# A routing stage whose order of experts, round count and weights are computed behind the token table

## The chip, the cores and the metric

The kernel runs on one core of a Trainium2 chip. The metric is the device time of one execution in microseconds. The kernel before takes 2070.55 us (median of 3 runs, 2066.29 to 2071.88).

## The reference

Two transformer blocks over 1024 tokens of width 1024. The first block has attention (a dilated and a neighbourhood branch) and a two-level mixture of 16 experts: the best of 4 groups, then the best 2 of its 4 experts. The second has three recurrent mixers and a feed-forward part. The change touches only the routing of the mixture:

```
g_weight, g_idx = lax.top_k(jax.nn.softmax(g_logits, axis=-1), 1)
e_in_group = jnp.take_along_axis(e_logits, g_idx[:, :, None], axis=1)[:, 0]
e_val, e_idx = lax.top_k(e_in_group, TOP_K_EXPERT)
e_weight = jax.nn.softmax(e_val, axis=-1) * g_weight
expert_id = g_idx * EXPERTS_PER_GROUP + e_idx
...
act = jax.nn.silu(gate) * up * combine[:, :, None].astype(x.dtype)
out = jnp.einsum('nef,efd->nd', act, w_down)
```

The kernel computes only the chosen experts: each expert gets the rows of the tokens that chose it.

## The kernel before

The attention output is projected in tiles of 128 tokens (`out_and_route`). Behind each tile the router's logits are made, and `route` handles the tokens in two batches of four tiles. From comparisons it makes one-hot rows `oh` (first and second choice), a running count of tokens per expert (`pk`, a matmul with a triangle of ones) and from it each token's rank `rk`. Two matmul groups (L899) then turn one-hot rows and ranks into the token table `tab`: for each expert (column) and each slot (row) the number of the token that sits there.

Behind the second batch come these pieces, all on VectorE:

- `sort_experts`: the load of each expert, its `place` when experts are sorted by load, the permutation `perm`, and `order`, the expert that stands at each place (L921 and L923).
- `sort_tokens`: `ix` from the table, `ixp` (table times permutation) and `idx`, the token numbers for each place (L936, L937); then `cmx` and `nround`, the number of rounds (L939 to L947).
- `route_weights`: expert ids `eid` and the softmax weights `wt` (L846 to L859).
- `slots_main`: `slot` and `wv`, where each token finds its results and with which weight (L956 to L976).

Two of these results start transfers. `idx` is read by GpSimd, which gathers token rows from DRAM by an indirect DMA (`xg<-xn_d,idx`, L1062): one for each tile of a job, into three buffers. `order` is read by SyncE into a register (L1054), which is the expert whose weights are then loaded (`wraw`, L227, 512 KB each): four units of gate and up weights and two of down weights for each expert, into four buffers. ScalarE casts each unit to a rounded high part `whi` (L237), VectorE subtracts to get the low part `wlo` (L238). A gathered tile is transposed on TensorE (L278) into two PSUM banks, copied by ScalarE (`XgH`, L280) and subtracted by VectorE (`XgL`, L281); each product is three matmuls (L260, L261, L262: high by high, low by high, high by low).

Every engine runs its instructions in one fixed order. That order is not the order of the code: when the program is built, instructions are ordered by what they depend on and by when their inputs are expected, so code of several functions is interleaved on VectorE. A read of a value that stands behind another instruction is what holds a piece back.

In the text below, W0 to W3 are the four gate and up units of the first expert, W4 and W5 the first two of the second expert, g0 and g1 the first two gathered tiles (both for the first expert), g2 the third.

Of the kernel before, what the change touches and what calls it, by code (L numbers as in the profile page):

```python
# [7 lines left out]
F32 = mybir.dt.float32  # L8
# [4 lines left out]
OP = mybir.AluOpType  # L13
AX = mybir.AxisListType
# [172 lines left out]
class K:  # L187
# [650 lines left out]
    def route_weights(self, wk, LG, oh):  # L838

        nc, V = self.nc, self.nc.vector  # L840
        e16 = self.rc[:, 144:160]
        w = wk.tile([128, 8, 20], F32, name="rwk")
        t3 = wk.tile([128, 8, 2, 16], F32, name="rt3")
        wg = w[:, :, 0:4]
        col = lambda i: w[:, :, 8 + i]
        V.tensor_tensor(t3, oh, e16[:, None, None, :].to_broadcast([128, 8, 2, 16]), op=OP.mult)  # L846
        V.tensor_reduce(self.eid, t3, axis=AX.X, op=OP.add)
        V.tensor_reduce(col(0), LG[:, :, 0:4], axis=AX.X, op=OP.max)
        V.tensor_tensor(wg, LG[:, :, 0:4], col(0).unsqueeze(2).to_broadcast([128, 8, 4]), op=OP.subtract)
        nc.scalar.activation(wg, wg, AF.Exp)  # L850
        V.tensor_reduce(col(3), wg, axis=AX.X, op=OP.add)
        V.tensor_tensor(t3, oh, LG[:, :, None, 4:20].to_broadcast([128, 8, 2, 16]), op=OP.mult)
        V.tensor_reduce(w[:, :, 9:11], t3, axis=AX.X, op=OP.add)
        V.tensor_tensor(col(4), col(2), col(1), op=OP.subtract)
        nc.scalar.activation(col(4), col(4), AF.Exp)
        V.tensor_scalar(col(5), col(4), 1.0, None, op0=OP.add)
        V.tensor_tensor(col(5), col(5), col(3), op=OP.mult)
        V.reciprocal(self.wt[:, :, 0], col(5))
        V.tensor_tensor(self.wt[:, :, 1], self.wt[:, :, 0], col(4), op=OP.mult)  # L859
# [46 lines left out]
    def sort_experts(self, wk, pc):  # L906

        nc, V = self.nc, self.nc.vector
        e16 = self.rc[:, 144:160]
        ab = lambda v: v.unsqueeze(2).to_broadcast([128, 16, 16])  # L910
        bb = lambda v: v[:, None, :].to_broadcast([128, 16, 16])
        load = wk.tile([128, 16], F32, name="load")
        key = wk.tile([128, 16], F32, name="key")
        V.scalar_tensor_tensor(key, pc, 16.0, e16, op0=OP.mult, op1=OP.subtract)
        t = wk.tile([128, 16, 16], F32, name="cmp")
        V.tensor_tensor(t, bb(key), ab(key), op=OP.is_gt)
        self.place = wk.tile([128, 16], F32, name="place")
        V.tensor_reduce(self.place, t, axis=AX.X, op=OP.add)
        perm = self.perm = wk.tile([128, 16, 16], F32, name="perm")
        V.tensor_tensor(perm, bb(self.place), ab(e16), op=OP.is_equal)  # L920
        V.tensor_tensor(t, perm, bb(e16), op=OP.mult)  # L921
        self.order = self.wp.tile([128, 16], I32, name="order")
        V.tensor_reduce(self.order, t, axis=AX.X, op=OP.max)  # L923
        V.tensor_copy(load, pc)
        self.load = load

    def sort_tokens(self, wk):

        V = self.nc.vector
        bb = lambda v: v[:, None, :].to_broadcast([128, 16, 16])  # L930
        self.idx = self.wp.tile([128, 2, 16], I32, name="idx")
        ix = wk.tile([128, 2, 16], F32, name="ix")
        ixp = wk.tile([128, 2, 16, 16], F32, name="ixp")
        V.tensor_tensor(ix, self.tab[:, :, 0:16], self.tab[:, :, 16:32], op=OP.add)
        for s in range(2):
            V.tensor_tensor(ixp[:, s], self.perm, bb(ix[:, s]), op=OP.mult)  # L936
            V.tensor_reduce(self.idx[:, s], ixp[:, s], axis=AX.X, op=OP.max)  # L937
        cm = wk.tile([128, 16], F32, name="cmx")
        V.tensor_scalar(cm, self.place, 0.5, None, op0=OP.is_ge)  # L939
        V.scalar_tensor_tensor(cm, self.place, NMORE + 0.5, cm, op0=OP.is_ge, op1=OP.add)  # L940
        V.scalar_tensor_tensor(cm, cm, 64.0, self.load, op0=OP.mult, op1=OP.add)
        V.tensor_reduce(cm[:, 0:1], cm, axis=AX.X, op=OP.max)
        V.tensor_scalar(cm[:, 1:2], cm[:, 0:1], 256.5, None, op0=OP.is_ge)
        for x in (512.5, 768.5, 1024.5):
            V.tensor_scalar(cm[:, 2:3], cm[:, 0:1], x, None, op0=OP.is_ge)
            V.tensor_tensor(cm[:, 1:2], cm[:, 1:2], cm[:, 2:3], op=OP.add)
        V.tensor_scalar(self.nround, cm[:, 1:2], 1.0, None, op0=OP.add)  # L947
# [1326 lines left out]
```

## Time and profile before

| | |
|---|---|
| median of the runs | 2070.55 us |
| the profiled execution's own time | 2072.83 us |
| its span | 2071.0 us |
| TensorE busy | 1933.4 us (93%) |
| VectorE busy | 1333.4 us (64%) |
| ScalarE busy | 931.1 us (45%) |
| mean DMA rate | 160 GB/s |
| mean granted clock | 0.97 |

The span is the profiled part of one execution; the time of the run is a little longer. Times below are microseconds from the span's start. An engine's busy share is a mean over stages with different limits, so the stage of the change is read by itself. In a row of instructions the bracket tells how long the engine stood idle before it and what ended the idle time.

### The profile page before, as it was taken

The page shows a single profiled execution, that of the slowest core. Times are in us where ns is not written, and L with a number is a line of the kernel's source. Part 1 is how long each engine was busy: PE and PEld are TensorE (multiplying, and loading weights), DVE is VectorE, ACT ScalarE, POOL GpSimd, SP SyncE. Part 2 cuts the span into 40 slices and gives each one's busy share as a digit, 9 for nine tenths or more (in the row PEclk, how much of TensorE's full clock was granted, in tenths as well). Part 3 has the DMA queues.
Part 4 walks back from the last instruction along what each step waited for, and adds up shares of the span by engine and source line. Part 5 has one row for each costly group of instructions (what it writes and reads, how often), then busy time and mean ns, then how long its engine had stood idle before and what let it go on. Part 6 is the DMA issues. An engine that isn't in the chain of part 4 may idle for free.

```text
span 2071.0 us, 27616 instructions
## 1 busy us (share of the span) xinstructions
PE 1933.4 (93%) x9481; PEld 1524.1 (74%) x9481; DVE 1333.4 (64%) x2670; ACT 931.1 (45%) x1648; POOL 731.3 (35%) x721
## 2 busy tenths in 40 slices
PE   8999999999899699995999989997999999999998
PEld 6877777776678577764887657675888888888886
DVE  4146667555657677766468278888667667675555
ACT  4245555444433477764422373454333333344344
POOL 2111102333442111105455224215677777740130
PEclk9999999999999799997999998998999999999999
DMA  6153322233332799966434246633335435458664
GB/s 243 61 130 101 89 76 79 87 103 102 114 127 83 251 315 317 319 239 219 166 97 68 72 165 206 201 133 133 141 134 180 148 135 182 149 193 305 195 190 167
DMA packets 161220, 332.23 MB, mean 160 GB/s; under 512 B 26256, under 2 KB 71600, under 8 KB 160560
## 3 DMA queue, kind: packets, MB, share of 16 engines
q1 hardware_dynamic: 139520, 260.64, 38.5%
q0 software_dynamic: 18848, 68.43, 10.1%
q10 hardware_dynamic: 2704, 1.31, 0.3%
q8 instruction: 77, 1.26, 0.3%
q14 instruction: 71, 0.58, 0.1%
HBM read 235.88 MB, written 84.93 MB: 155 GB/s over the span
## 4 chain that ended last, share of the span: by engine, by line
PE 40%; DVE 6%; POOL 3%; issue 3%; DMA 2%; ACT 1%; SPq 0%; POOLq 0%; DVEq 0%; ACTq 0%
PE pd L260 3%; PE pd L262 3%; PE pd L261 3%; PE pb L260 3%; PE pb L262 3%; PE pb L261 3%; PE pa L262 2%; PE pa L260 2%; PE pc L260 2%; PE pc L261 2%; PE pc L262 2%; PE pa L261 2%; PE pvg L260 1%; PE pvg L262 1%; PE pvg L261 1%
## 5 line engine op out<-in xcount | busy, mean ns | idle before, releaser
L2001 ACT CAST whi<-wraw 128x1024 fp32r<-128x1024 f32 x137 | 134.7, 984 | 273.7 <-PE pd L262 89.1
L2002 DVE TENSOR_TENSOR wlo<-wraw,whi 128x1024 fp32r<-128x1024 f32 x137 | 178.3, 1303 | 78.1 <-ACT whi L2001 75.9
L237 ACT CAST whi<-wraw 128x1024 fp32r<-128x1024 f32 x122 | 127.9, 1049 | 120.1 <-PE pp L261 37.8
L260 PE MATMUL pp<-XH,whi 128*128 128x512 f32 x416 | 167.2, 402 | 1.0 <-DVE kk L404 0.9
L262 PE MATMUL pp<-XH,wlo 128*128 128x512 f32 x416 | 165.8, 398 | 0.0
L261 PE MATMUL pp<-XL,whi 128*128 128x512 f32 x416 | 165.3, 397 | 0.0
L238 DVE TENSOR_TENSOR wlo<-wraw,whi 128x1024 fp32r<-128x1024 f32 x96 | 117.3, 1223 | 52.0 <-ACT whi L237 50.8
L238 POOL TENSOR_TENSOR wlo<-wraw,whi 128x1024 fp32r<-128x1024 f32 x26 | 63.1, 2427 | 172.6 <-ACT whi L237 163.6
L260 PE MATMUL pd<-whi 128*128 128x512 f32 x308 | 120.2, 391 | 1.0 <-DVE res L2171 0.9
L261 PE MATMUL pd<-wlo,whi 128*128 128x512 f32 x308 | 120.3, 390 | 0.5 <-DVE wlo L2002 0.5
L262 PE MATMUL pd<-whi,wlo 128*128 128x512 f32 x308 | 120.1, 390 | 0.0
L1062 POOL DMA_INDIRECT xg<-xn_d,idx x25 | 31.8, 1272 | 180.6 <-PE pt L278 141.3
L260 PEld LDWEIGHTS pp<-XH,whi 128*128 128x128 f32 x416 | 78.8, 189 | 19.5 <-issue 3.6
L262 PEld LDWEIGHTS pp<-XH,wlo 128*128 128x128 f32 x416 | 78.8, 189 | 15.5 <-issue 1.4
L261 PEld LDWEIGHTS pp<-XL,whi 128*128 128x128 f32 x416 | 78.8, 190 | 15.1 <-issue 1.5
L531 ACT ACTIVATE PP<-PP,stat 128x256 f32<-128x256 f32 x128 | 64.5, 504 | 39.6 <-DVE stat L529 37.5
L529 DVE CUSTOM_DVE_ANT_0 PP<-sp,bias 128x256 f32<-128x256 f32 x128 | 52.9, 422 | 25.5 <-PE sp L527 21.3
L281 DVE TENSOR_TENSOR XL<-pt,XH 128x512 fp32r<-128x512 f32 x32 | 20.7, 686 | 75.3 <-ACT XH L280 75.3
L260 PEld LDWEIGHTS pd<-whi 128*128 128x128 f32 x308 | 57.8, 188 | 14.3 <-DVE res L2171 1.7
L261 PEld LDWEIGHTS pd<-wlo,whi 128*128 128x128 f32 x308 | 57.9, 188 | 13.2 <-DVE wlo L2002 1.2
L262 PEld LDWEIGHTS pd<-whi,wlo 128*128 128x128 f32 x308 | 57.8, 188 | 12.1
L2173 POOL TENSOR_TENSOR res<-res,p 128x512 f32<-128x512 f32 x12 | 23.7, 2008 | 116.4 <-DVE res L2171 116.4
(638 smaller groups left out, 5774.8 us busy)
## 6 DMA issues: line engine op xcount, KB each, us to landing
wraw<-in_wgu_dram SPq DMA_DIRECT2D x64, 512.0 KB, 5.1
wraw<-in_wup_dram SPq DMA_DIRECT2D x44, 512.0 KB, 4.9
wraw<-act_d SPq DMA_DIRECT2D x77, 256.0 KB, 2.8
wraw<-in_wdn_dram SPq DMA_DIRECT2D x32, 512.0 KB, 4.9
fX<-in_wdown_dram SPq DMA_DIRECT2D x22, 512.0 KB, 4.5
wdt_d<-fX SPq DMA_DIRECT2D x44, 256.0 KB, 2.3
wraw<-wdt_d SPq DMA_DIRECT2D x44, 256.0 KB, 3.0
act_d<-ft SPq DMA_DIRECT2D x33, 256.0 KB, 2.3
```

Of the source, the lines that this page charges most:

```text
L237: nc.scalar.copy(hi, raw)
L238: (eng or nc.vector).tensor_tensor(lo, raw, hi.bitcast(F32), op=OP.subtract)
L260: nc.tensor.matmul(out, lh, rh, start=start, stop=False, **kw)
L261: nc.tensor.matmul(out, lh, rl, start=False, stop=False, **kw)
L262: nc.tensor.matmul(out, ll, rh, start=False, stop=stop, **kw)
L281: nc.vector.tensor_tensor(XL[:, 4 * q:4 * q + 4, c], pt, h.bitcast(F32), op=OP.subtract)
L529: nc.vector.tensor_tensor_reduce(out=PP[j // 4][:, j % 4], in0=so, in1=bs, op0=OP.add, op1=OP.min, scale=1.0, scalar=3e38, accum_out=nm)
L531: nc.scalar.activation(PP[j // 4][:, j % 4], PP[j // 4][:, j % 4], AF.Exp, bias=nm, scale=-1.0, accum_out=stt[:, stj[0], 1, stj[1]:stj[1] ...
L1062: nc.gpsimd.indirect_dma_start(out=xg[0:n], out_offset=None, in_=self.xn_d, in_offset=bass.IndirectOffsetOnAxis(ap=idx[0:n, s, p:p + 1], a ...
L2001: nc.scalar.copy(h[:, 0:n], src)
L2002: nc.vector.tensor_tensor(l[:, 0:n], src, h[:, 0:n].bitcast(F32), op=OP.subtract)
L2173: nc.gpsimd.tensor_tensor(r, r, p1[:, t], op=OP.add)
```

## The change

`order` is no longer computed in `sort_experts`, between `perm` and the ranks. It is computed in `sort_tokens`, behind the index reductions. One-column copies tie the pieces together: a column of the tile that the product for `order` will overwrite, and one of `cm` (the round count), are first written from `ixp`, so both pieces depend on the index work; and a column of `t3` in `route_weights` is first written from `order`, so expert ids and weights come behind it. The copied values are overwritten before they are used.

```
--- before.py
+++ after.py
@@ route_weights
         t3 = wk.tile([128, 8, 2, 16], F32, name="rt3")
+        V.tensor_copy(t3[:, 0, 0, 0:1], self.order[:, 0:1])
         wg = w[:, :, 0:4]
@@ sort_experts
         V.tensor_tensor(perm, bb(self.place), ab(e16), op=OP.is_equal)
-        V.tensor_tensor(t, perm, bb(e16), op=OP.mult)
         self.order = self.wp.tile([128, 16], I32, name="order")
-        V.tensor_reduce(self.order, t, axis=AX.X, op=OP.max)
         V.tensor_copy(load, pc)
-        self.load = load
+        self.load, self.cmp = load, t
@@ sort_tokens
             V.tensor_tensor(ixp[:, s], self.perm, bb(ix[:, s]), op=OP.mult)
             V.tensor_reduce(self.idx[:, s], ixp[:, s], axis=AX.X, op=OP.max)
-        cm = wk.tile([128, 16], F32, name="cmx")
+
+        t, cm = self.cmp, wk.tile([128, 16], F32, name="cmx")
+        for o in (t[:, 0, 0:1], cm[:, 0:1]):
+            V.tensor_copy(o, ixp[:, 1, 15, 15:16])
+        V.tensor_tensor(t, self.perm, bb(self.rc[:, 144:160]), op=OP.mult)
+        V.tensor_reduce(self.order, t, axis=AX.X, op=OP.max)
         V.tensor_scalar(cm, self.place, 0.5, None, op0=OP.is_ge)
```

What stands on VectorE around the token table before (`rk` ranks, `tr` the rank comparisons for the table, `tab` the table, `ix` and `ixp` its permuted form, `cmx` the round count, `eid` and `rwk` ids and weights):

```order
L823 TENSOR_REDUCE rk<-rt_6470 128x8 [waits DVE_49]
L921 TENSOR_TENSOR cmp<-perm,rc 128x256 [waits DVE_49]
L888 TENSOR_SCALAR tr<-tc_5614,rk 128x256 [waits DVE_49]
L923 TENSOR_REDUCE order<-cmp 128x16 [waits DVE_49]
L888 TENSOR_SCALAR tr<-tc_5614,rk 128x256 x7
L939 TENSOR_SCALAR cmx<-place 128x16
L846 TENSOR_TENSOR rt_6561<-roh,rc 128x256
L940 SCALAR_TENSOR_TENSOR cmx<-place,cmx 128x16 [waits DVE_49]
L902 TENSOR_TENSOR tab<-tab,ptab 128x64 [waits PE_49]
L941 SCALAR_TENSOR_TENSOR cmx<-cmx,load 128x16 [waits DVE_49]
L847 TENSOR_REDUCE eid<-rt_6561 128x16
L934 TENSOR_TENSOR ix<-tab 128x32 [waits DVE_49]
```

and in the same place now, up to the new `order`:

```order
L889 TENSOR_SCALAR tr<-tc_5614,rk 128x256 [waits DVE_49]
L889 TENSOR_SCALAR tr<-tc_5614,rk 128x256 x7
L903 TENSOR_TENSOR tab<-tab,ptab 128x64 [waits PE_49]
L933 TENSOR_TENSOR ix<-tab 128x32 [waits DVE_49]
L935 TENSOR_TENSOR ixp<-perm,ix 128x256 [waits DVE_49]
L935 TENSOR_TENSOR ixp<-perm,ix 128x256
L936 TENSOR_REDUCE idx<-ixp 128x16 [waits DVE_49] x2
L940 COPY cmp<-ixp 128x1
L940 COPY cmx<-ixp 128x1
L941 TENSOR_TENSOR cmp<-perm,rc 128x256 [waits DVE_49]
L943 TENSOR_SCALAR cmx<-place 128x16 [waits DVE_49]
L942 TENSOR_REDUCE order<-cmp 128x16 [waits DVE_49]
```

Round count, ids and `order` have left the stretch between the ranks and `idx`; `order` is now behind `idx`. One small reduce of `rwk` (L852) has moved ahead of the first `tr`.

On SyncE, the loads behind the first expert's four units W0 to W3, before (the first load here is W4; `norm_final_g` and `attn_norm` are two gain rows for the next stage):

```order
L227 DMA wraw<-in_wgu_dram 128x1024 [waits DMAHW7_49,DMAHW3_49,DVE_49]
L227 ISA
L227 DMA wraw<-in_wgu_dram 128x1024 [waits DMAHW0_49,DMAHW4_49,DVE_49,Activation_49]
L227 ISA
L227 DMA wraw<-in_wdn_dram 128x1024 [waits DMAHW5_49,DMAHW1_49,DVE_49]
L255 DMA norm_final_g<-in_norm_final_g_dram 128x1024 [waits DMAHW6_49,PE_49]
L255 DMA attn_norm_6703<-in_attn_norm_dram 128x1024
```

and now:

```order
L227 DMA wraw<-in_wgu_dram 128x1024 [waits DMAHW7_49,DMAHW3_49,DVE_49]
L255 DMA norm_final_g<-in_norm_final_g_dram 128x1024 [waits DMAHW4_49,PE_49]
L255 DMA attn_norm_6706<-in_attn_norm_dram 128x1024 [waits DMAHW5_49]
L227 ISA
L227 DMA wraw<-in_wgu_dram 128x1024 [waits DMAHW6_49,DMAHW0_49,DVE_49]
L227 ISA
L227 DMA wraw<-in_wdn_dram 128x1024 [waits DMAHW1_49,DVE_49]
```

The two gain rows have moved ahead of W5 and of the first expert's down weights. On GpSimd and TensorE the order is unchanged; on ScalarE one small exponential now stands ahead of the casts of W0 and W1.

## Rows read from the trace of the kernel before

**Rows 1.** The page, part 1: busy us, share of the span, instructions.

```profile
PE 1933.4 (93%) x9481; PEld 1524.1 (74%) x9481; DVE 1333.4 (64%) x2670; ACT 931.1 (45%) x1648; POOL 731.3 (35%) x721
```

**Rows 2.** Table by stretch: from:to, length, busy per engine, clock, DMA share, GB/s.

```profile
682.00:697.00 15.00, 4.55 (x20) 3.64 (x19) 12.38 (x52) 5.88 (x8) 5.55 (x4) 0.50 0.96 340
697.00:760.00 63.00, 62.16 (x285) 47.89 (x284) 43.88 (x56) 40.89 (x62) 8.64 (x7) 0.97 0.88 298
```

**Rows 3.** Timeline of TensorE: start, us, line, tiles, count, idle before and releaser.

```profile
680.43 1.60 PE L899 MATMUL ptab<-tw,tr 128*128 128x32 bf16 x15 [0.32 <-DVE tr L888]
690.92 1.94 PE L278 MATMUL pt<-ident,xg 128*128 128x128 f32 x8 [8.89 <-DMA xg<-xn_d,idx]
...
695.46 1.94 PE L278 MATMUL pt<-ident,xg 128*128 128x128 f32 x8 [1.56 <-DMA xg<-xn_d,idx]
697.06 0.78 PE L262 MATMUL pg<-whi,XgL 128*128 128x512 f32 x1
```

**Rows 4.** Timeline of GpSimd: issue of the gathers g0 and g1.

```profile
684.82 1.27 POOL L1062 DMA_INDIRECT xg<-xn_d,idx  x1 [12.55 <-DVE cmx L946]
686.39 2.06 POOL L1062 DMA_INDIRECT xg<-xn_d,idx  x1 [0.30 <-issue]
```

**Rows 5.** DMA issues, us to landing: W0, W3, down weights, g0, g1.

```profile
wraw<-in_wgu_dram SPq DMA_DIRECT2D x1, 512.0 KB, 3.6
...
wraw<-in_wgu_dram SPq DMA_DIRECT2D x1, 512.0 KB, 6.7
...
wraw<-in_wdn_dram SPq DMA_DIRECT2D x1, 512.0 KB, 12.3
...
xg<-xn_d,idx POOLq DMA_INDIRECT x1, 6.0
...
xg<-xn_d,idx POOLq DMA_INDIRECT x1, 8.9
```

**Rows 6.** Timeline of SyncE's queue: issue of W0 to W3; then of W3 and W4.

```profile
681.25 1.94 SPq L227 DMA_DIRECT2D wraw<-in_wgu_dram  x4
...
682.86 5.13 SPq L227 DMA_DIRECT2D wraw<-in_wgu_dram  x2
```

**Rows 7.** Timeline of ScalarE: casts of W0 and W3, first XgH, cast of W5.

```profile
684.83 1.04 ACT L237 CAST whi<-wraw 128x1024 fp32r<-128x1024 f32 x1 [8.58 <-DMA wraw<-in_wgu_dram]
...
689.59 1.04 ACT L237 CAST whi<-wraw 128x1024 fp32r<-128x1024 f32 x1 [0.27 <-DMA wraw<-in_wgu_dram]
692.05 0.59 ACT L280 CAST XgH<-pt 128x512 fp32r<-128x512 f32 x1 [1.41 <-PE pt L278]
...
704.02 1.05 ACT L237 CAST whi<-wraw 128x1024 fp32r<-128x1024 f32 x1 [1.79 <-PE pg L262]
```

**Rows 8.** Timeline of VectorE: order, table, index, then W3's split and XgL.

```profile
679.24 0.41 DVE L921 TENSOR_TENSOR cmp<-perm,rc 128x256 f32<-128x256 f32 x1
679.58 0.28 DVE L888 TENSOR_SCALAR tr<-tc,rk 128x256 bf16<-128x256 bf16 x1
679.77 0.41 DVE L923 TENSOR_REDUCE order<-cmp 128x16 int32<-128x256 f32 x1
680.10 1.45 DVE L888 TENSOR_SCALAR tr<-tc,rk 128x256 bf16<-128x256 bf16 x7
...
682.07 0.22 DVE L902 TENSOR_TENSOR tab<-tab,ptab 128x64 f32<-128x64 f32 x1
...
682.89 0.75 DVE L936 TENSOR_TENSOR ixp<-perm,ix 128x256 f32<-128x256 f32 x2
683.56 0.74 DVE L937 TENSOR_REDUCE idx<-ixp 128x16 int32<-128x256 f32 x2
...
692.09 1.22 DVE L238 TENSOR_TENSOR wlo<-wraw,whi 128x1024 fp32r<-128x1024 f32 x1
693.22 1.28 DVE L281 TENSOR_TENSOR XgL<-pt,XgH 128x512 fp32r<-128x512 f32 x2
```

**Rows 9.** Table by stretch as in rows 2: the rate with full queues.

```profile
686.00:688.00 2.00, 0.00 (x0) 0.00 (x0) 2.00 (x12) 1.17 (x2) 1.70 (x2) 0.50 1.02 408
```

## The prediction

> **What bounds the kernel now.** I read the whole first (the span), then a table of busy time by stage, then the one seam that the change touches, engine by engine. TensorE is busy for 1933 of 2071 us [rows 1], so an edit elsewhere counts only where TensorE stands still. One such place is the seam between routing and experts: from 682 to 697 us it is busy for 4.55 of 15 us, at the lower clock (0.50 granted, 1.2 GHz), while the DMA engines are 96% busy; from 697 to 760 it is busy for 62.16 of 63 us [rows 2]. The reader should see in these two rows that the seam ends when TensorE gets its stream, and that whatever moves 697 moves all that follows.
>
> What does TensorE wait for? Its rows show three steps [rows 3]. The last matmul of the token table runs until 682.03. The first gathered tokens (tile g0) land at 690.8 and are transposed; two products follow. Then the transposes of the second tile (g1) wait until 695.46, again for a DMA, and at 697.06 the third product starts; from there TensorE does not stop. So g1's landing sets 697.06. The first gather is issued at 684.82 and the second at 686.39 [rows 4], and they land 6.0 and 8.9 us later [rows 5]. Nearly the whole way they share the DMA engines with the first expert's four weight units (W0 to W3), whose issue starts at 681.25 [rows 6].
>
> The second thing to see is ScalarE's order [rows 7]: four casts of W0 to W3 (684.83 to 689.59) stand ahead of the first copy of gathered tokens, XgH, at 692.05. The last of these casts begins when W3 lands, 682.86 + 6.7 = 689.56 [rows 5, 6], and the tokens come later, so nothing is lost there today. That order is fixed, so a late W3 would hold the tokens up.
>
> **The change, part by part.** *Ahead of the index.* Two instructions of `order` leave the chain: L921 holds VectorE from 679.24 to 679.58 (0.34 us until the next starts), L923 from 679.77 to 680.10 (0.33) [rows 8]. One small reduce of the weights comes in ahead; it reads an eighth of what L923 reads, so I estimate 0.1 of the latter's 0.33. Between the table's sum (L902, 682.07) and the index reductions (L937, 683.56) VectorE spent 1.49 us, of which 0.82 lay ahead of the ixp products; that held four small instructions of round count, expert ids and weights beside ix. Now only ix stands there: L902 took 0.22 and an ix like it some 0.2, so about 0.44 in place of 0.82. Together 0.34 + 0.33 - 0.10 + 0.38 = 0.95 us; I take 0.9. The index is complete at 684.30 - 0.9 = 683.4 and the gathers are issued at 683.9 and 685.5.
>
> *Behind the index.* `order` was complete at 679.77 + 0.41 = 680.18 [rows 8]. Now it stands behind the last index reduction: that starts at about 683.0 and holds VectorE 0.33 (as L923 did); a one-column copy, no longer than the 0.22 of L902, I take 0.15; the product, about 0.43 with its hand-over; the reduce, 0.41. It ends at 684.3, so 4.1 us later. SyncE reads `order` before any weight load of the first expert; from 680.18 to the first load it took 1.07 us. So the four loads start at 681.25 + 4.14 = 685.4. The other moved items (round count, ids, softmax weights; three one-column copies more) run on VectorE between 684.3 and the first weight cast, where nothing but wv, slot and the loop count, all read after the experts, depends on them; I cost them at nothing. That cover ends when W0 is cast: they would then push the first wlo, which is needed only after W3's tokens below.
>
> *What is late next.* The gain at the gathers is worth something only if W3 is there. One transfer of 512 KB (0.524 MB) at 408 GB/s, as from 686 to 688 us [rows 9], takes 1.285 us; W0 landed 3.6 us after its issue with the engines to itself [rows 5], so 2.3 us of that is not data. Lower bound for W3: only the weights ahead of it, 685.4 + 2.3 + 4 x 1.285 = 692.8. Upper bound: all three first gathers ahead too, 685.4 + 2.3 + 7 x 1.285 = 696.7. In between, the old lag of W3 (6.7 us from an issue at 682.86, [rows 5, 6]) moved along gives 693.7, but that lag held only part of g0. Now g0 and g1 are issued at 683.9 and 685.5, so both fall into the weights' time: six transfers, 695.4. I take this value.
>
> The Trainium skill, page "DMA: Bandwidth & Descriptors", section "Where 436 GB/s comes from", says that transfers between HBM and SBUF are bound at about 358 GB/s per core. By it six transfers would take 8.8 us, W3 would land at 696.5 and the sum below would be 4.0 us. This trace differs, with 408 GB/s [rows 9], so the sum stays with the rows.
>
> From W3 on ScalarE casts it (1.04), then copies the two halves of g0; VectorE splits W3 (1.22, next start 1.13 later) and then both halves of XgL, 1.28 for the two, as at 692.09 and 693.22 [rows 7, 8]. XgL's first half ends at W3 + 1.1 + 1.15 + 0.7 = W3 + 3.0. Only then is a bank free for g1's transposes, and in the old run the third product started 1.6 after these (695.46 to 697.06, [rows 3]). So the unbroken stream starts at W3 + 4.6: 700.0 in place of 697.06, a loss of 2.9 us; with the bounds 697.4 (0.3 lost) and 701.3 (4.2 lost). Below nothing only if the rest of the chain from W3 is shorter than 4.3 us.
>
> *Later loads.* The two gain rows (norm_final_g, attn_norm) now stand ahead of the second expert's second unit W5. W5 is issued behind the split of W1. W1 lands two to four transfers in, 690.3 to 692.8; with 1.04 for the cast and 1.22 for the split that is 692.6 to 695.1, in the middle 693.9. With the longest lag of this stretch, 12.3 us (the down weights, [rows 5]), W5 lands at 706.2. It was cast at 704.02 [rows 7]; 2.9 later is 706.9. So it is just hidden, and I add nothing. Round-count and `order` reads on SyncE lie between loads that wait for VectorE anyway.
>
> *Sum.* Profiled execution 2072.83 us (span 2071.0 and 1.83 around it) + 2.9 = 2075.7. The median of the runs shown is 2070.55, 2.28 under the profiled one; on that footing 2073.5 us.
>
> **Rivals.** *A, the gather stays the bound.* If the weights cost the gathers little and W3 lands by 691, g1 sets the start: issued at 685.5, with the lag of g0 (6.0) to its own (8.9) it lands at 691.5 to 694.4, and the stream starts 1.6 later, 693.1 to 696.0. That is 1.1 to 4.0 us gained, in the middle 2068.0. For it: TensorE's row names the gather and not the weights [rows 3]. Against it: W3 at 691 is below the lower bound of 692.8.
>
> *B, the queue behind the late weights becomes the bound, slower.* The loads of W4, two gain rows and W5 follow one another 4 us late on a DMA system that is 96% busy. If W5's lag grows past 13.0 us (706.9 - 693.9), TensorE stands before the second expert's second unit, us for us; at 17.0 it is 4 more, 6.9 in all, 2077.5. For it: the lags already grew from 3.6 to 12.3 within this stretch [rows 5]. Against it: 0.88 DMA share after 697 [rows 2] leaves room to catch up.
>
> *C, it does not do what it says.* If the earlier index and the later weights cancel (W3 at 692.4, the break-even of 697.06 - 4.6), nothing moves: 2070.6. For it: the lower bound of W3 is 0.4 us from there. Against it: the gathers' 1 MB must then wait behind all weights.
>
> **How the numbers follow.** A measurement of this kernel tells about 0.3% (6.2 us) from no change; the three runs shown span 5.6 us. Forecast 0.60, A 0.17, C 0.13, B 0.10. The forecast, C and most of A lie within 0.3%. Faster than 2064.3 needs A at its far end (2066.6) and 2 us of spread: 0.06. Slower than 2076.8 is B, and a forecast at its upper bound (2074.8) with spread: 0.12. Same: 0.82. For the range, the low end takes A's far end, 2066.5; the high end B's 2077.5 with 1.5 of spread, 2079. The likeliest case's own range is 2070.9 to 2074.8.
>
> **What would show it.** In the changed profile: the first gather at 683.9 and the first weight load at 685.4; g1 landed before TensorE asks for it; the first XgH copy right behind the fourth weight cast and not behind a transpose; the idle time before the unbroken stream ended by ScalarE or VectorE and no longer by a gather; and the stream from 700. I am wrong if W3 lands before 692.4 (then C or A), if g1's transposes still wait for their DMA, or if TensorE waits for weights between 700 and 720 (B).

## The result: slower by 0.6%, and the profile after

The changed kernel takes 2081.32 us (median of 7 runs, 2075.15 to 2091.38), the kernel before 2070.45 us beside it (7 runs, 2066.29 to 2074.61): 1.0059 times as long, 95% interval [1.0042, 1.0076], some 11 us. I forecast 2073.5, no change that can be measured. The profiled execution of the changed kernel took 2075.15 us (span 2073.0), the shortest of its seven, so its span beside that of before (2071.0) shows less than the medians do. Therefore I read the seam itself, and count from `perm` (L921 after, L920 before), an instruction just ahead of the place where the two kernels part. It starts at 676.27 after; before, at 678.71:

```profile
678.71 0.42 DVE L920 TENSOR_TENSOR perm<-place,rc 128x256 f32<-128x256 f32 x1
```

Busy time has hardly changed against [rows 1]; from the page of the changed kernel, the same columns:

```profile
PE 1929.4 (93%) x9481; PEld 1517.8 (73%) x9481; DVE 1332.1 (64%) x2673; ACT 931.4 (45%) x1648; POOL 724.2 (35%) x721
```

No work was added that matters: this is waiting. The table by stretch, against [rows 2], shows where TensorE lost its work: 1.94 us of it up to 697, where before there were 4.55, and some standing in the next stretch too. The last row is the mean rate over the weights' way, for [rows 9].

```profile
682.00:697.00 15.00, 1.94 (x8) 1.57 (x8) 9.04 (x44) 3.86 (x5) 3.37 (x4) 0.50 0.91 314
697.00:760.00 63.00, 60.62 (x277) 46.78 (x278) 42.28 (x54) 39.79 (x61) 7.96 (x7) 0.96 0.83 282
...
684.00:696.00 12.00, 1.94 (x8) 1.57 (x8) 6.04 (x32) 3.35 (x4) 1.84 (x2) 0.50 0.99 348
```

TensorE's timeline of the changed kernel answers to [rows 3]:

```profile
686.06 1.94 PE L278 MATMUL pt<-ident,xg 128*128 128x128 f32 x8 [7.01 <-DMA xg<-xn_d,idx]
698.08 0.80 PE L260 MATMUL pg<-whi,XgH 128*128 128x512 f32 x1 [10.08 <-ACT XgH L280]
...
699.46 1.97 PE L278 MATMUL pt<-ident,xg 128*128 128x128 f32 x8 [0.16 <-DVE XgL L281]
701.08 0.78 PE L262 MATMUL pg<-whi,XgL 128*128 128x512 f32 x1
```

The reader should see the gain and the loss one above the other. The first tokens are there at 686.06, 9.79 behind `perm` where before it was 12.21 (0.9 of this is the earlier index, most of the rest g0's shorter way, below). Then TensorE stands for 10.08 us, and what it waits for is no longer a transfer by name but ScalarE's XgH. ScalarE's timeline, against [rows 7], says why:

```profile
689.46 1.04 ACT L237 CAST whi<-wraw 128x1024 fp32r<-128x1024 f32 x1 [4.35 <-DMA wraw<-in_wgu_dram]
691.69 1.04 ACT L237 CAST whi<-wraw 128x1024 fp32r<-128x1024 f32 x1 [1.19 <-DMA wraw<-in_wgu_dram]
694.75 1.04 ACT L237 CAST whi<-wraw 128x1024 fp32r<-128x1024 f32 x1 [2.01 <-DMA wraw<-in_wgu_dram]
696.50 1.05 ACT L237 CAST whi<-wraw 128x1024 fp32r<-128x1024 f32 x1 [0.70 <-DMA wraw<-in_wgu_dram]
697.45 1.06 ACT L280 CAST XgH<-pt 128x512 fp32r<-128x512 f32 x2
```

All four casts wait for weights, and the token copies, whose input had been transposed by 688, go out straight behind the fourth. VectorE's timeline (against [rows 8]) shows where the weights' delay begins:

```profile
676.27 0.42 DVE L921 TENSOR_TENSOR perm<-place,rc 128x256 f32<-128x256 f32 x1
...
680.25 0.74 DVE L936 TENSOR_REDUCE idx<-ixp 128x16 int32<-128x256 f32 x2
...
681.54 0.42 DVE L942 TENSOR_REDUCE order<-cmp 128x16 int32<-128x256 f32 x1
```

`order` stands behind the index now, and SyncE (against [rows 6]) issues W0 to W3 behind it:

```profile
683.03 1.94 SPq L227 DMA_DIRECT2D wraw<-in_wgu_dram  x4
```

GpSimd's timeline (against [rows 4]) shows the gathers g0 to g3:

```profile
681.51 1.06 POOL L1066 DMA_INDIRECT xg<-xn_d,idx  x1 [11.67 <-DVE cmp L941]
682.88 0.95 POOL L1066 DMA_INDIRECT xg<-xn_d,idx  x1 [0.30 <-issue]
684.14 0.94 POOL L1066 DMA_INDIRECT xg<-xn_d,idx  x1 [0.30 <-issue]
688.28 0.91 POOL L1066 DMA_INDIRECT xg<-xn_d,idx  x1 [3.20 <-PE pt L278]
```

Two gathers more than I counted (g2 at 684.14, g3 at 688.28) are on their way before W3 is there: g3's row names TensorE's transposes of g0 as its releaser, and those ran early because g0 was early. The DMA issues, with the microseconds to landing (W0, W3, g0, g1, g3), against [rows 5]:

```profile
wraw<-in_wgu_dram SPq DMA_DIRECT2D x1, 512.0 KB, 6.4
...
wraw<-in_wgu_dram SPq DMA_DIRECT2D x1, 512.0 KB, 11.8
...
xg<-xn_d,idx POOLq DMA_INDIRECT x1, 4.4
...
xg<-xn_d,idx POOLq DMA_INDIRECT x1, 8.0
...
xg<-xn_d,idx POOLq DMA_INDIRECT x1, 7.5
```

g3 lands at 688.28 + 7.5 = 695.8, ahead of W3 at 696.4. It is a tile of 64 rows, half a transfer, so the gathers made 3.5 transfers of 0.524 MB ahead of W3, not two. And they are not all. From 683 to 696.5, W0's issue to W3's landing, the queue of the loads (q1) and that of the gathers (q0) moved:

```profile
q1 hardware_dynamic: 723, 2.67, 56.2%
q0 software_dynamic: 512, 1.84, 41.0%
```

The columns after the colon are packets, MB and share. W0 to W3 are 2.10 MB; the other 0.57 on q1 belong to W4 and the gain rows, which are issued before W3 has landed. So 4.5 MB moved where I had counted six transfers, 3.15 MB.

### The profile page after: what moved, and what is told of

It is laid out like the page before. It is cut to its first block, busy times and chain, and to the rows that moved or that the text cites. A ratio compares the mean times of both kernels' runs of the same rounds, so it can differ in the third digit from the quotient of the medians.

```text
span 2073.0 us, 27616 instructions
## 1 busy us (share of the span) xinstructions
PE 1929.4 (93%) x9481; PEld 1517.8 (73%) x9481; DVE 1332.1 (64%) x2673; ACT 931.4 (45%) x1648; POOL 724.2 (35%) x721
## 4 chain that ended last, share of the span: by engine, by line
PE 39%; DVE 6%; issue 3%; POOL 2%; DMA 2%; ACT 2%; SPq 0%; POOLq 0%; DVEq 0%; ACTq 0%
PE pd L260 3%; PE pd L261 3%; PE pd L262 3%; PE pb L260 3%; PE pb L262 3%; PE pb L261 3%; PE pa L262 2%; PE pa L260 2%; PE pc L262 2%; PE pc L261 2%; PE pc L260 2%; PE pa L261 2%; PE pvg L260 1%; PE pvg L262 1%; PE pvg L261 1%
## 5 line engine op out<-in xcount | busy, mean ns | idle before, releaser
L262 PEld LDWEIGHTS pp<-XH,wlo 128*128 128x128 f32 x416 | 79.0, 190 | 15.8 <-issue 1.4
L260 PE MATMUL pg<-whi,XgH 128*128 128x512 f32 x136 | 57.7, 425 | 10.6 <-ACT XgH L280 10.6
```

The costliest lines, as they stand in the source:

```text
L260: nc.tensor.matmul(out, lh, rh, start=start, stop=False, **kw)
L262: nc.tensor.matmul(out, ll, rh, start=False, stop=stop, **kw)
```

## The experiments

The theory: ScalarE runs the four weight casts ahead of the first token copy, so the late `order` holds the tokens up through W3's landing, and that is late because of what shares the DMA engines with it. Rivals: the new place of the gain rows or the extra instructions cost the time; the one profile of before was not typical; the gathers, and not the weights, set the seam.

**The changed kernel and the kernel before, each once more, unedited.**

> The changed kernel once more, unedited, so that its seam and its later stages can be read in a second execution. Start theory (the time is lost where the fourth weight unit W3 lands late and the first token copy stands behind its cast): 2081 us, W3 lands about 14 us after order is complete and the unbroken stream starts 4.6 us behind it, whatever the total. Later theory (half of the 11 us is lost behind the seam, in a weight queue that stays late): the seam loses 6 to 7 us as in the first profile, and 4 us more are found between 700 and 930 us as waits of TensorE for weights.

> The kernel before once more, unedited, for a second trace of it. The first trace came from an execution 4.5 us above the median of its 23 runs. Account by two parts (seam and spread): in an execution near the median the seam is as long as in the first trace (18.4 us from perm to the unbroken stream, within 0.5), and the missing 4 us lie in front of it or behind the experts, so that the loss of 10 us is 6 at the seam and 4 in later stages of the changed kernel. Rival: the seam itself is shorter by 3 us or more in a typical execution (the second gather lands earlier), and the whole loss lies there.

The changed kernel took 2078.47 us (6 runs), 1.005 [1.0032, 1.0069]; the kernel before 2068.99 (10 runs), 0.9997 [0.9979, 1.0016]. The loss stands: in the second profile of the changed kernel the unbroken stream starts 24.18 us behind `perm`, in the first 24.81. But the second profile of before is not like the first. TensorE of this second run of before, where `perm` is at 678.57:

```profile
690.69 1.94 PE L278 MATMUL pt<-ident,xg 128*128 128x128 f32 x8 [8.79 <-DMA xg<-xn_d,idx]
...
693.92 1.60 PE L278 MATMUL pt<-ident,xg 128*128 128x128 f32 x8 [0.25 <-DVE XgL L281]
695.28 0.48 PE L262 MATMUL pg<-whi,XgL 128*128 128x512 f32 x1
695.60 0.40 PE L260 MATMUL pg<-whi,XgH 128*128 128x512 f32 x1
```

And GpSimd's issue of g1 there:

```profile
686.26 0.95 POOL L1062 DMA_INDIRECT xg<-xn_d,idx  x1 [0.30 <-issue]
```

The second gather's issue took 0.95 us where [rows 4] have 2.06, g1 is not waited for, the stream starts 16.71 behind `perm` in place of 18.35, and TensorE is at its upper clock at once (granted 1.00 from 695 to 698, 0.40 us for a product; the first trace has 0.50 up to 700, and 0.63 us). At the 3720th matmul that makes 3.1 us. So the rival on the profile holds this far: the seam that I had measured from was slower than this one, and g1's wait, on which my "what bounds it" rested, is not always there. Which of the two seams is usual, two profiles don't say; both executions took longer than the median of their kernel's runs (2072.83 against 2070.55 us, 2071.83 against 2068.99).

**`order` early again, the rest of the change kept.**

```
     perm = ... is_equal
+    V.tensor_tensor(t, perm, bb(e16), op=OP.mult)
     self.order = ...
+    V.tensor_reduce(self.order, t, axis=AX.X, op=OP.max)
...
-    V.tensor_tensor(t, self.perm, ...)      (behind the index)
-    V.tensor_reduce(self.order, t, ...)
```

> order is made in sort_experts again, between the ranks; round count, ids and softmax weights stay behind the index. Start theory: W0 to W3 start 4 us earlier again, the gather of the second tile sets the start, index 0.5 us earlier than before: 2069 to 2071 us. Rival (what hurts are the small instructions moved behind the index): no better than 2077 us.

2072.09 us (12 runs), 1.0016 [1.0000, 1.0031]: most of the loss is gone, so the instructions that stay behind the index are not what costs it, and nothing is gained over before. Its ScalarE, the fourth cast and the first token copy (`perm` at 675.54):

```profile
686.27 1.04 ACT L237 CAST whi<-wraw 128x1024 fp32r<-128x1024 f32 x1 [0.26 <-DMA wraw<-in_wgu_dram]
688.91 0.59 ACT L280 CAST XgH<-pt 128x512 fp32r<-128x512 f32 x1 [1.59 <-PE pt L278]
```

And its TensorE:

```profile
691.67 1.97 PE L278 MATMUL pt<-ident,xg 128*128 128x128 f32 x8 [0.91 <-DVE XgL L281]
693.29 0.78 PE L262 MATMUL pg<-whi,XgL 128*128 128x512 f32 x1
```

The copies wait for transposes again and not for a cast. The gather is issued 5.76 behind `perm` (6.10 in the second run of before), but its tokens reach TensorE 12.25 behind (12.12): behind W0 to W3 the earlier index buys nothing.

**The other way round: the kernel before with only `order` moved behind the index.**

```
-    V.tensor_tensor(t, perm, bb(e16), op=OP.mult)
-    V.tensor_reduce(self.order, t, ...)
...                                         (behind the index reductions)
+    V.tensor_copy(t[:, 0, 0:1], ixp[:, 1, 15, 15:16])
+    V.tensor_tensor(t, self.perm, bb(self.rc[:, 144:160]), op=OP.mult)
+    V.tensor_reduce(self.order, t, axis=AX.X, op=OP.max)
```

> The kernel before with order alone made behind the index; round count, ids and weights stay where they were. Here only three weight casts stand ahead of the first token copy, and W3 is loaded behind the two gain rows. Start theory: the start hangs on W2 in place of W3, about 2 us earlier: 2076 to 2080 us. Rival (late weights are harmless as long as the index is early): 2070 us.

2079.36 us (6 runs), 1.006 [1.004, 1.0081]; stream 25.32 behind `perm`. This one move, with the order that the build makes of it, gives the whole loss. That order is not quite the changed kernel's: three casts and not four stand ahead of the tokens, and SyncE has the gain rows ahead of W3 (issued at 686.36 and 687.00; W0 at 684.84). The 2 us that I expected from the shorter row of casts did not come: W2 lands 13.1 us behind W0's issue. ScalarE of this run, the cast of W2, then the tokens:

```profile
697.96 1.04 ACT L237 CAST whi<-wraw 128x1024 fp32r<-128x1024 f32 x1 [1.64 <-DMA wraw<-in_wgu_dram]
698.91 1.06 ACT L280 CAST XgH<-pt 128x512 fp32r<-128x512 f32 x2
```

**The changed kernel with the token copies ahead of the casts of W1 to W3** (those casts' output tiles first get one column from the token tile, which orders them).

```
     hi = pool.tile(...)
+    if self.hold is not None:
+        nc.vector.tensor_copy(hi[:, 0:1], self.hold)
     nc.scalar.copy(hi, raw)
...                                         (first job, behind unit 0)
+    self.hold = X[0][1][:, 4, 0:1].bitcast(F32)
```

> The changed kernel, with a column of the casts of W1 to W3 first written from the split of the first tokens, so that ScalarE copies the tokens of both first tiles right behind the cast of W0. The two gain rows come ahead of W4. Start theory: the start now hangs on W0 and on the second gather, at about 697 us in the time of the kernel before: 2069 to 2073 us. Later theory: the loads are as late as in the changed kernel, so at least 2075 us. Rival (DMA alone): as the changed kernel, 2081 us.

2074.37 us (12 runs), 1.0029 [1.0012, 1.0046]. ScalarE, with the casts of W0 and W4 and the tokens between (`perm` at 676.54):

```profile
687.90 1.04 ACT L240 CAST whi<-wraw 128x1024 fp32r<-128x1024 f32 x1 [2.52 <-DMA wraw<-in_wgu_dram]
688.85 1.06 ACT L283 CAST XgH<-pt 128x512 fp32r<-128x512 f32 x2
...
701.43 1.05 ACT L240 CAST whi<-wraw 128x1024 fp32r<-128x1024 f32 x1 [4.07 <-DMA wraw<-in_wgu_dram]
```

TensorE there, at the start of the stream and at its first break:

```profile
693.20 0.78 PE L265 MATMUL pg<-whi,XgL 128*128 128x512 f32 x1
...
708.31 0.46 PE L1080 MATMUL pt<-ident,xg 64*128 64x64 f32 x4 [2.42 <-DVE XgL L284]
```

With `order` as late as in the change the stream starts 16.66 behind `perm`, like before's 16.71: the stop is the place of the casts, not the lateness as such. Part of it comes back at the second expert. SyncE issues the gain rows at 685.54, ahead of W4, the cast of W4 waits 4.07 us, and the next tokens stand behind a late cast again.

**The same with the gain rows loaded in the second expert** (their tiles first written from that expert's token tile).

```
-    self.g1, self.g2 = (self.bcast_row(...) ...)     (first expert)
...
+    if e == 1:
+        self.g1, self.g2 = (self.bcast_row(..., after=self.gh) ...)
```

> e4_tokens_first, with the two gain rows loaded behind the split of the second expert's tokens, so that they leave the queue ahead of the second expert's weights. In e4 TensorE lost 5.8 us between its matmuls 3720 and 3760, at the second expert's token transposes. Queue theory (the gain rows made those weights late, ScalarE stood at their casts and the token copies behind them): the 5.8 us come back, 2067 to 2070 us. Rival (ScalarE's order alone, six casts ahead of the copies): no change, 2074 us.

2074.97 us (10 runs), 1.0038 [1.0024, 1.0051]: no better. In its trace the loss between the 3720th and the 3760th matmul fell from 5.5 to 1.6 us, but that execution (2069.82) is the shortest of its ten; the median does not bear it out. Inconclusive for the second expert. For W3 the trace does say something: it lands 12.8 us behind W0's issue, with the gain rows ahead of W4 it was 13.0. So the gain rows are not what makes W3 late; without them W4 (issued at 690.57) is still on its way beside it.

**The changed kernel with g2 and g3 held until W3 has landed** (one column of W3's cast goes into their tile first; in the code, the fourth unit moves ahead of these gathers).

```
     xg = wk.tile(...)
+    if self.ghold is not None:                       (a column of W3's whi)
+        V.tensor_copy(xg[0:n, 0:1], self.ghold[0:n])
     nc.gpsimd.indirect_dma_start(out=xg[0:n], ...)
```

> The changed kernel, with the gathers for the second expert (g2, g3) held until the fourth weight unit is cast, by a column written from that cast. Start theory with the transfers ahead as the cause of W3's lateness: 0.79 MB leave the way, at 350 to 408 GB/s 1.9 to 2.3 us, so W3 lands and the stream starts 2 us earlier than in the changed kernel: 2076 to 2077 us. Rival (mixed queues are slow whatever is ahead, or g2 is not served first): no change, 2079 us. A late g2 would show as a wait before the second expert's transposes.

2077.23 us (11 runs), 1.0038 [1.0023, 1.0054]; the medians alone do not tell it from the change, as the intervals overlap. ScalarE, casts of W0 and W3, then the tokens (W0's issue at 681.06, `perm` at 674.31):

```profile
685.27 1.04 ACT L238 CAST whi<-wraw 128x1024 fp32r<-128x1024 f32 x1 [2.12 <-DMA wraw<-in_wgu_dram]
...
692.20 1.05 ACT L238 CAST whi<-wraw 128x1024 fp32r<-128x1024 f32 x1 [0.30 <-DMA wraw<-in_wgu_dram]
693.15 1.06 ACT L281 CAST XgH<-pt 128x512 fp32r<-128x512 f32 x2
```

W3 lands 11.1 us behind W0's issue; in the change it is 13.4 in the first profile and 12.8 in the second. The two gathers, 0.79 MB, are worth 1.7 to 2.3 us. What is left is still more than the six transfers of my sum: from 681 to 692.2 the trace has 3.89 MB, some 0.7 of it W4 and the gain rows.

**Can the early index be used? `order` early, loads of W1 to W3 held until the index is complete** (their tiles first get a column of it), the casts behind the tokens, the gain rows late.

```
+    self.idx_done = ...tile([128, 1]);  V.tensor_copy(self.idx_done, self.idx[:, 1, 15:16])
...
-            unit(src, 1, X, pg)
+            unit(src, 1, X, pg, self.idx_done)       (and units 2 and 3)
```

> order is made early (as in e2), W0 is loaded early, W1 to W3 only once the index is complete, tokens are copied ahead of the casts of W1 to W3, the gain rows come late (as in e7), round count and weights stay behind the index. Start theory: the two first gathers meet one weight unit at a time, so the unbroken stream starts 14 to 15 us behind perm in place of 18.4, 3 to 4 us gained at the seam: 2064 to 2067 us if the experts keep it. Later theory (the experts are held by their weights): the gain is given back, 2068 us or more.

2071.86 us (12 runs), 1.0013 [0.9998, 1.0028]; the stream starts 16.73 behind `perm`, as in the second run of before, not the 14 to 15 that I expected. Then with the loads held until g0 has landed, on this kernel and, in a second run, on the kernel before:

```
             unit(src, 0, X, pg)
+            if main and i == 0:
+                self.hold = X[0][1][:, 4, 0:1].bitcast(F32)
+                late = self.xg0            (a column of g0's tile)
-            unit(src, 1, X, pg)
+            unit(src, 1, X, pg, late)      (and units 2 and 3)
```

> The kernel with order made early, the index behind the table without it, the casts of W1 to W3 behind the token copies and the gain rows late, in which now the loads of W1 to W3 are issued only when the first gather (g0) has landed, so that beside W0 the gathers have the DMA engines alone. My theory (the seam is set by the bytes ahead of the last landing that TensorE needs): g0 lands 4.4 to 5 us behind its issue in place of about 6 to 6.4, g1 within 5.5 in place of 8, and the first product of the unbroken stream starts 13 to 14.5 us behind perm, in place of 16.7 in both the kernel before and this kernel with the loads early. W1, issued some 10.3 behind perm, lands 3.6 to 4.5 later and is cast and split by about 16.5, while the products of W0 last to about 18, so it is hidden. Median 2065.5 to 2069.5, 0 to 4 us under the kernel before, as an early start of the experts is partly given back later (two runs that started 3 us early gave back 4.5 and 2.9 us). Rival (the gathers are bound by themselves, not by the weights beside them): g0 lands 6 behind its issue as ever, the weights come later, and the stream breaks before W1's or W2's products by 2 to 4 us: 2072 to 2076.

> The kernel before with one thing altered: the loads of W1 to W3 are issued only when the first gather has landed, and their casts stand behind the first token copies. Order, index and gain rows as before. My theory: the same 2 to 3 us at the seam as in the run sent with it, less the 0.9 us that the later index costs: stream 14 to 15.5 us behind perm in place of 16.7, median 2066.5 to 2070. Rival: gathers not faster without the weights beside them, W1 late: 2072 to 2076.

The first: 2072.72 us (12 runs), 1.0008 [0.9996, 1.0019], not told apart from before. Its TensorE (`perm` at 675.79):

```profile
688.96 1.91 PE L283 MATMUL pt<-ident,xg 128*128 128x128 f32 x8
690.52 0.78 PE L267 MATMUL pg<-whi,XgL 128*128 128x512 f32 x1
...
697.90 0.50 PE L265 MATMUL pg<-whi,XgH 128*128 128x512 f32 x1 [1.04 <-ACT whi L240]
699.16 0.51 PE L266 MATMUL pg<-wlo,XgH 128*128 128x512 f32 x1 [0.76 <-DVE wlo L241]
```

The gathers are faster alone (g0 4.5 us, g1 5.6), and the stream starts 14.73 behind `perm`, 2 us sooner; 6 us on it breaks for W2, which comes too late. My theory had the first half, the rival the second. The other: 2079.12 us (12 runs), 1.0039 [1.0024, 1.0055], slower, and outside both of my ranges. Its stream starts 15.18 behind `perm`, sooner than before too, but the cast of W1 then waits 7.43 us for its load: SyncE has the gain rows ahead of W1.

```profile
694.98 0.33 SPq L258 DMA_DIRECT2D norm_final_g<-in_norm_final_g_dram  x1
695.45 0.34 SPq L258 DMA_DIRECT2D attn_norm<-in_attn_norm_dram  x1
696.40 3.21 SPq L228 DMA_DIRECT2D wraw<-in_wgu_dram  x4
```

I had not followed where those rows would stand. No version beats the kernel before.

**All of them side by side.** How much later the 3760th matmul starts (well inside the first experts' work), counted from the last matmul of the token table and against the second run of before, and how the medians differ, in us:

```
                               at matmul 3760   median - before
change, first and second profile     9.4, 9.0        10.9, 10.2
order late only                         10.5              11.1
change, g2 and g3 held                   8.4               7.8
g0 first, on before                      8.2               8.3
change, tokens first                     6.9               6.1
  and gain rows late                     3.3               5.5
g0 first, order early                    5.0               1.9
order early                              1.7               3.8
order early, loads at the index          1.0               2.4
first profile of before                  3.2
```

The seam, in one execution each, gives the medians to within some 3 us, over nine kernels. What lies behind it is not settled to that fineness. By the 4720th matmul, at the end of the experts, the second run of before stands 1.4 us behind the first, ahead of which it was by 3.2, and the change 6.6 and 5.9 us behind the second run of before, 8.0 and 7.4 behind the first. So 3 to 4 of the 10 to 11 us by which the medians differ are not located in these traces.

## Why the prediction was wrong

- *The index 0.95 us earlier*: right. It is complete 680.99 - 676.27 = 4.72 behind `perm`, before 5.59.
- *`order` 4.1 us later, the first load with it*: right. It ends 5.69 behind `perm`, before 1.47; W0 is issued 6.76 behind, before 2.54: 4.22 both times.
- *The tokens held up by the fourth cast, the stream at W3 + 4.6*: right. 701.08 - 696.4 = 4.7. Rivals A and C (a gather still sets the seam; no effect) fell with it.
- *W3 at 695.4, ten us behind W0's issue*: this failed. It came 13.4 behind (12.8 in the second profile). I counted six transfers in "In between", 3.15 MB; 4.5 MB moved before W3 was there. Of the 1.4 MB more, 0.79 are g2 and g3, which had been issued before W3 was there, and 0.57 are W4 and the gain rows, issued behind W3. With these bytes my own lag and rate give 2.3 us + 4.5 MB at 408 GB/s = 13.3 us. Within 0.7 us they do so in other traces too: 13.3 from 4.47 MB in the second profile of the change (measured 12.8), 11.8 from 3.89 MB with g2 and g3 held (11.1), 8.7 from 2.60 MB in the first trace of before (8.3). So what failed is the count. That the two gathers are part of it, the run with them held shows; the part of W4 and the gain rows rests on the bytes alone, as no run held both back. In the first profile's own terms the seam got 24.81 - 18.35 = 6.5 us longer, not 2.9; the 3.5 between are W3's.
- *The lag of 2.3 us and the rate of 408 GB/s*: neither holds by itself, and that the two together fit is luck. W0, from which I took the lag, did not have the engines to itself: W1 to W3 were issued before it landed. In the change the first packet moves 0.24 us behind W0's issue, as g0 is on its way already. And 408 is the best of the four rates from 682 to 690, while W0 to W3 were on their way (256, 377, 408, 311); the mean from 684 to 696 is 348 in the changed kernel. The lag was too long, the rate too high.
- *The weighing of the rate*: the Trainium skill, page "DMA: Bandwidth & Descriptors", section "Where 436 GB/s comes from", has about 358 GB/s per core for transfers between HBM and SBUF. I set it aside for 408. The mean of 348 agrees with it, but the changed kernel also has 418 GB/s from 690 to 692 and 408 over the six microseconds from 696 to 702 (gain rows among the loads), so as a bound it did not hold here. Six transfers at that figure put W3 1.1 us later, by the prediction's own estimate. 3.4 were missing, so the choice between the two rates did not make the miss. The first trace of before had the mean of 684 to 696 as well, had I asked for the whole stretch:

```profile
684.00:696.00 12.00, 3.52 (x13) 2.64 (x14) 10.40 (x42) 5.47 (x7) 5.55 (x4) 0.50 0.97 347
```

- *The first gather's way*: I had the 1 MB of g0 and g1 take their turn among the weights. With the weights later, g0 landed 4.4 us behind its issue, not 6.0, but no product could use it.
- *The upper bound of 2074.8 and the footing on the medians*: too low by the rest. "Profiled execution + 2.9" took the one seam of before for typical; the repeat is 3.1 us shorter at the 3720th matmul, and against it the change loses 9.3 us there, not 6.2. The rest of the 10.9 us between the medians has no cause shown.
- *Later loads at nothing*: they became no wait of their own in the change, but W4 and the gain rows moved 0.57 MB before W3 landed, which belongs to W3's term. Where other parts were moved, loads behind W3 did become a wait (tokens first; g0 first on before), so rival B named a real mechanism, for other kernels than this one.
- *"Nearly the whole way" beside W0 to W3*: a misreading. W3 had landed at 689.56; g1, which landed at 695.3, shared its last six microseconds with loads and gathers issued behind W3. The same kind of traffic was missing from the sum for W3.
- *The range*: its high end was built from B, a case on the far side, while the forecast's own upper bound (4.2 us, "all three first gathers ahead too") was 2.3 us under what came. A bound from all that can be on the way before W3 lands (W0 to W4, four gathers, two gain rows: 5.5 MB, with the same lag and rate) would have put W3 15.8 us behind W0's issue, and held it.

## What to carry to other kernels

An engine that takes its work in a fixed order turns a late load into a wait of whatever stands behind it: before a producer is moved back, follow its load to the cast and see what is queued behind it. Size the landing by all the bytes that can be on the way by then, those that an earlier step sets free and those issued behind the load too, and try lag and rate together on a landing that the trace already has. And take a seam from more than one execution where microseconds decide: here one profile of before differed from the next by 3 of them.

## What the runs showed of the hardware

Gathers with no weight load beside them were no fast stream: in the kernel before with g0 first (the last run above), from 692 to 694 us, when only gathers were on their way, the engines were 87% busy at 299 GB/s, where [rows 9] have 408 with weight loads among them.

```profile
692.00:694.00 2.00, 0.30 (x2) 0.34 (x3) 1.93 (x10) 0.00 (x0) 1.72 (x1) 0.50 0.87 299
```

Their landing shortens all the same: g0 takes 4.4 to 4.6 us in the runs where its way is its own for the most part, 6.0 in [rows 5]. And the clock is not granted alike at the same point: products right behind g1's transposes took 0.40 us in the second run of before, at a granted clock of 1.00 (2.4 GHz), and 0.63 in the first, at 0.50 (1.2 GHz). Ahead of these transposes TensorE had stood idle for 0.25 us in the second run and for 1.56 in the first [rows 3].
